# A two-layer hybrid backbone: the mixers as 570 named units, emitted in the order of a written list

## The chip, the cores and the metric

The kernel runs on one core of one Trainium2 chip. The metric is the device time of one execution, in microseconds (us), as the median of several runs; lower is better.

## What is computed

Two layers of a diffusion backbone work on 512 latent tokens and 256 context tokens of width 1024. Each layer has a mixer and a channel part, both wrapped in norms, modulation and gates:

```python
h = rmsnorm(x, norm_g[0]) * (1 + sc1[:, None]) + sh1[:, None]
qa, ka, va, qr, kr, vr, gr, z, xbc, dt = jnp.split(h @ w_in, split_idx, axis=-1)
att, att_c = attention_mixer(qa, ka, va, ...)      # 6 heads of 64, softmax over 768 keys
ret, ret_c = retention_mixer(qr, kr, vr, gr, ...)  # 4 heads, both directions, chunks of 128
ssd, ssd_c = ssd_mixer(z, xbc, dt, ...)            # 6 heads, convolution of 5 taps, chunks of 128
o = jnp.concatenate([att, ret, ssd], axis=-1) @ w_out
x = x + g1[:, None] * rmsnorm(o, norm_g[1])
h2 = rmsnorm(x, norm_g[2]) * (1 + sc2[:, None]) + sh2[:, None]
x = x + g2[:, None] * rmsnorm(squared_relu_mlp(h2, w_ff1, w_ff2), norm_g[3])
```

The context tokens go through the same steps in the first layer; in the second they only serve as keys, values and first states. All data are float32. Large products are made from three products of split operands (a high part and a rest).

## The kernel before

Tokens lie in six tiles of 128 (four latent, two context). The function `mixers(l, ...)` writes the whole mixer of one layer, and it does so in five stretches of Python code, one after the other:

- **Projections for keys and values, and the convolution.** `kvp` holds the products for attention keys, values and step sizes. Then seven groups of 128 convolution channels follow (`conv_chunk`, groups 3, 4, 5, 6, 0, 1, 2): products into `xbc`, a copy into `cin`, four taps in `acc` (L696), a tanh `th`, and for groups 0 to 4 the transposes `xt` back to tokens. `kv_post` (norm and rotation of the keys, in two halves) stands behind group 4, `decays` behind group 5.
- **State-space heads.** `ssd_head_a` makes the decay matrix `tb` of a head (scalar, vector and GpSimd work), `ssd_head_b` multiplies it (`yi`), and `ssd_state` takes one step of the state in both directions: a weighting `vw` (L784), the product with the state before (`in`), and the sums `ds` (L797). One tile of the projections `qap` and `zp` is written between the pieces.
- **Gate and norm** of the state-space output, through DRAM.
- **Attention.** For each head and pair of query tiles: scores `s`, maximum, softmax `P`, transposes `pt`, product with the values `pv`, and a store (L966). One tile of `krvp`, `qgp` or one step of the modulation `mq` (first layer only) is written after each pair.
- **Retention.** For each of four heads: transposes of keys and queries (`dTkr`, `dTqr`), scores `rs`, chunk sums `rd`, the state `rst` (a chain of ten VectorE instructions, L1050 and L1052), outputs `ry` (L1056, L1057), a group norm. Transposes of finished outputs (`sT`) and the first products of the output projection (`op`) are written between.

Memory is handed out in rings: a tag such as `t3` has four buffers, `u3` six, `m6` three, `n9` two, and PSUM has two buffers for each of `pa`, `pb`, `pc`. A tile that is written later in the code gets the next buffer of its ring when the one before is released.

All loads and stores stand on SP's queue, in order. Each engine works through its own instructions in order. That order is not simply the order in which the code writes the instructions: the compiler's planner reads what was written, with its dependencies and buffers, and puts instructions that it takes to be ready ahead of earlier ones; among ready ones, the one written first goes first.

Of the kernel before, what the change touches and what calls it, by code (L numbers as in the profile page):

```python
# [9 lines left out]
F32 = mybir.dt.float32  # L10
# [10 lines left out]
D = 1024  # L21
# [21 lines left out]
def shape_constants():  # L43
# [16 lines left out]
    # query minus key in a chunk; steps from the chunk before to a query, for both directions  # L60
# [3 lines left out]
    return cst, rel  # L64

# [15 lines left out]
def tile_hybrid_backbone(  # L81
# [120 lines left out]
    def wraw(src, shape, name):  # L202
        """one half of a unit: at most 1024 elements a partition"""
# [6 lines left out]
    def wunit(src, shape, name, lo_eng=None, pool=None):  # L210
        """src: function (first row block, row blocks) -> list of (AP, first column, columns)"""
# [13 lines left out]
    def wcols(w, k0, cols):  # L225
        """row blocks from k0 on; cols: list of (column in w, column in the unit, columns)"""
# [44 lines left out]
    def mod_cols(l, sec, q, nrow):  # L271
        """section of 512 columns of the modulation, as per-feature columns; q: [nrow, 512] in SBUF"""
# [75 lines left out]
    def mod_sums(l, sec, acc, raw=None):  # L348
        """the same, with the sums over the chunks off the tensor engine; acc [128, 2, 512]"""
# [22 lines left out]
    def cond_cols(n):  # L372
        """silu of both conditionings: [partition, chunk of 128 / n features, stream], the same on n groups of partitions"""
# [15 lines left out]
    def mod_groups(secs, acc, cs):  # L389
        """sections [(layer, section)] side by side on groups of partitions; acc [128, 2, 512]"""  # L390
# [27 lines left out]
    def gate_row(pool, l, which, stream):  # L418
        """(gate * norm_g) of one stream on every partition; which 0: mixer, 1: channel"""
# [16 lines left out]
    def modulate(q, xv, tt, l, which, hT, lo_eng=None, ks=(0, KC), cut=KC // 2):  # L436
        """q, xv [128, chunk, token]: q * A + B -> xv, and its parts into tile tt of hT"""
# [13 lines left out]
    def norm_tile(src, xh, tt, l, which, hT, lo_eng=None, half_bank=None):  # L451
        """src [128, D]; xh a scratch [128, D]; writes tile tt of hT (hi, lo)"""
# [12 lines left out]
    def mm3(o, a, b, first, last):  # L465
        """o += a^T b for split operands a = (hi, lo), b = (hi, lo)"""
# [18 lines left out]
    def tiles(pool, name, n=6):  # L485
        """tokens of tile tt: [:, tt] = [chunk, token]"""
# [14 lines left out]
    def mixers(l, mp, hT, alloc_mix, kvw=None):  # L501
# [48 lines left out]
        def rope(st, t, nh):  # L550
            """rotate st [128, nh * 64] (one tile of latent tokens) in place"""
# [7 lines left out]
        def qk_norm(q, st, t, nh, goff, ms=None):  # L559
            """q [128, nh * 64] in PSUM -> st: rmsnorm a head, gain, rotation; with ms only the sums of squares"""  # L560
# [17 lines left out]
        # ---- steps of the state-space heads, attention keys and values  # L578
# [13 lines left out]
        run(tm_group("kv", 268, [(KA, 0, 256), (DT0, 256, 12)], 6, c_kv, (pB, pC), kvw[:1]))  # L592
        if l:
            # out of the memory of the weights, once that of the mixers is free
            for i in range(2):
                G.tensor_copy(kvt[:, 3 * i : 3 * i + 3], kvr[i])
                kvr[i] = kvt[:, 3 * i : 3 * i + 3]

        def kv_post():
            for i in range(2):  # L600
                ts = slice(3 * i, 3 * i + 3)
                nc.sync.dma_start(tv(vad)[:, ts, :], kvr[i][:, :, 128:256])
                sq = t3([128, 3, 2, 64], f"sq{i}")
                kv = kvr[i][:, :, 0:128].rearrange("p t (h d) -> p t h d", d=64)
                ms = sm.tile([128, 3, 2], F32, tag="km", name=f"km{l}{i}")
                rs = sm.tile([128, 3, 2], F32, tag="kr", name=f"kr{l}{i}")
                S.activation(sq, kv, AF.Square)
                V.tensor_reduce(ms, sq, AX.X, ALU.add)
                V.tensor_scalar(ms, ms, 1.0 / 64, EPS, ALU.mult, ALU.add)
                rsqrt(rs.rearrange("p a b -> p (a b)"), ms.rearrange("p a b -> p (a b)"), 6, "kv")  # L610
                for h in range(2):
                    k = kv[:, :, h, :]
                    G.tensor_tensor(k, k, bc(par[:, P_KG : P_KG + 64], 1, 3), ALU.mult)
                    G.tensor_tensor(k, k, bc(rs[:, :, h], 2, 64), ALU.mult)
                for t in range(3 * i, min(4, 3 * i + 3)):
                    rope(kvr[i][:, t % 3, 0:128], t, 2)
                nc.sync.dma_start(tv(kad)[:, ts, :], kvr[i][:, :, 0:128])

        def mod_secs(*secs):
            if l == 0:  # L620
                for s in secs:
                    yield from (mod_whole if s in (6,7,8,9,) else mod_split)(0, s, lambda shape, name: mp.tile([128, 512], F32, tag="fcol", name=name)[: shape[0]])
# [5 lines left out]
        mods_gen = mod_secs(*range(4, 10))  # L628
# [10 lines left out]
        def decays():  # L639
            """decays of the state-space heads"""  # L640
# [3 lines left out]
            V.scalar_tensor_tensor(la, dtv, -1.0, bc(ea, 1, 6), ALU.mult, ALU.mult)  # L644
            lav = la.rearrange("p a b -> p (a b)")
# [14 lines left out]
            V.tensor_scalar(ncol, fcol[:, :, 0:12], -1.0, None, ALU.mult)  # L660
            G.memset(frow[64:128].bitcast(F32), 0.0)
# [5 lines left out]


        # ---- convolution channels
# [4 lines left out]
        cwu = {}  # L674

        def conv_chunk(j):
            on = wc or j < 5
            h, lo = cwu[j]
            cin = t3([128, 776], "cin")
            acc = t3([128, 776], "acc")  # L680
            n = 772 if on else 512
            G.memset(cin[:, 0:2], 0.0)
            G.memset(cin[:, 514:518], 0.0)
            if on:
                G.memset(cin[:, 774:776], 0.0)
            for c0, t0, t1 in ((2, 0, 512), (518, 512, 768))[: 2 if on else 1]:
                q = pB([128, 512], f"xbc{l}{j}{t0}")[:, : t1 - t0]
                qv = q.rearrange("p (t c) -> p t c", c=128)
                ts = slice(t0 // 128, t1 // 128)
                for k in range(KC):  # L690
                    mm3(qv, (h[:, k, :], lo[:, k, :]), (hh[:, ts, k, :], hl[:, ts, k, :]), k == 0, k == KC - 1)
                S.activation(cin[:, c0 : c0 + t1 - t0], q, AF.Copy)  # L692
# [13 lines left out]
            if j < 5:  # L706
                q = pA([128, 6, 128], f"xt{l}{j}")
                for t in range(6):
                    transpose(q[:, t, :], dst[:, tcol(t) : tcol(t) + 128])
                o = xs_tok[:, :, j * 128 : (j + 1) * 128] if j < 3 else b_tok[:, :, (j - 3) * 128 : (j - 2) * 128]  # L710
                S.activation(o, q, AF.Copy)

        for js in ((3, 4), (5, 6), (0, 1), (2,)):
            h, lo = kvw[1] if js[0] == 3 and len(kvw) > 1 else xbc_unit(l, js)
            for i, j in enumerate(js):
                cwu[j] = (h[:, :, i * 128 : (i + 1) * 128], lo[:, :, i * 128 : (i + 1) * 128])
                conv_chunk(j)
                if j == 4:
                    kv_post()
                if j == 5:  # L720
                    decays()

        # ---- state-space heads
# [11 lines left out]

        mats = {}

        def ssd_head_a(h):
            g = h // 3
            gf = gfb[g]  # L740
            a = t3([128, 6, 128], f"a{h}")
            for d in range(2):
                r = 6 * d + h
                qf = pA([128, 6, 128], f"F{l}{h}{d}")
                qv = qf.rearrange("p a b -> p (a b)")
                oh = onehot[:, r : r + 1].broadcast_to([128, 128])
                T.matmul(qv[:, 0:512], oh, frow[:, 0:512], start=True, stop=True)
                if wc:
                    T.matmul(qv[:, 512:768], oh, frow[:, 512:768], start=True, stop=True)
# [724 lines left out]
```

## Time and profile before

| what | us |
|---|---|
| runs | 1890.38, 1890.81, 1883.89 |
| median | 1890.38 |
| span of the profiled execution, first to last instruction | 1880.8 |
| PE busy in it | 1753.1 |
| VectorE (DVE) busy in it | 1219.7 |
| ScalarE (ACT) busy in it | 703.0 |
| GpSimd (POOL) busy in it | 369.1 |
| mean granted clock of TensorE, share of full | 0.972 |

A separate total time of the profiled execution is not recorded: its span stands for it. The lowest run is 3.1 us above that span and the median 9.6 us. Busy time is the time in which an engine has an instruction under way; matmuls are pipelined, so their records overlap and the mean duration of one is longer than the distance from one to the next. A wait is idle time of an engine just before an instruction, put down to what ended it.

### The profile page before, as it was taken

To read this page: it belongs to the slowest core of one execution; us is meant where nothing else is said; L and a number is where in the kernel's file an instruction comes from. 1 tells how busy PE (TensorE), PEld (TensorE's weight loads), DVE (VectorE), ACT (ScalarE), POOL (GpSimd) and SP (SyncE) were. 2 spreads that over 40 slices of the span, in tenths; PEclk is the share of its full clock that TensorE was granted. 3 is DMA by queue.
4 is the path that set the end of the run, shared out by engine and by line. 5 is a ranking of instruction groups with operands and counts; after the bars stand their busy time and mean duration, and the time that the engine had idled before them with its cause. 6 is when DMAs were issued, how large, how long until landed. Compare 5 with 4: busy or idle time off the path is not lost. (4 is left out here: it accounts for less than half of the span.)

```text
span 1880.8 us, 24641 instructions
## 1 busy us (share of the span) xinstructions
PE 1753.1 (93%) x8991; PEld 1443.0 (77%) x8991; DVE 1219.7 (65%) x2462; ACT 703.0 (37%) x1267; POOL 369.1 (20%) x391
## 2 busy tenths in 40 slices
PE   6987999997999999999999979888987999999998
PEld 2877977655878888888888868777866788888886
DVE  5868985664668566566566586788876654444445
ACT  5543376652461111201201275433772532222222
POOL 0047232313001100100100132553022021111112
PEclk9999999997999999999999999999996999999999
DMA  8410243366444334434434433224324432222332
GB/s 274 124 52 32 89 149 104 104 182 184 146 135 136 124 101 132 125 107 123 126 105 118 152 123 91 65 71 124 100 73 110 147 122 90 90 90 91 102 105 95
DMA packets 189078, 217.00 MB, mean 115 GB/s; under 512 B 67667, under 2 KB 142237, under 8 KB 188957
## 3 DMA queue, kind: packets, MB, share of 16 engines
q1 hardware_dynamic: 188956, 215.43, 37.8%
q8 instruction: 71, 1.16, 0.2%
q14 instruction: 51, 0.41, 0.1%
HBM read 189.66 MB, written 25.72 MB: 115 GB/s over the span
## 5 line engine op out<-in xcount | busy, mean ns | idle before, releaser
L467 PE MATMUL f<-h_h,wh_f 128*128 128x512 f32 (+1 forms) x800 | 280.3, 351 | 1.4 <-ACT h_h L448 1.4
L469 PE MATMUL f<-h_h,wl_f 128*128 128x512 f32 (+1 forms) x800 | 281.0, 352 | 0.0
L468 PE MATMUL f<-h_l,wh_f 128*128 128x512 f32 (+1 forms) x800 | 280.1, 350 | 0.8 <-DVE h_l L449 0.8
L1299 POOL TENSOR_TENSOR r<-r 128x768 f32<-128x768 f32 (+1 forms) x64 | 93.8, 1466 | 847.4 <-ACT r L1298 837.8
L467 PE MATMUL f<-wh_g,uh 128*128 128x512 f32 x640 | 253.0, 396 | 4.1 <-DVE acc L1327 1.7
L468 PE MATMUL f<-wl_g,uh 128*128 128x512 f32 x640 | 252.6, 395 | 0.0
L469 PE MATMUL f<-wh_g,ul 128*128 128x512 f32 x640 | 251.8, 394 | 0.0
L221 ACT ACTIVATE wh_f<-wr_f 128x1024 fp32r<-128x1024 f32 x64 | 66.5, 1055 | 377.2 <-PE f L469 164.4
L1329 DVE TENSOR_TENSOR acc<-acc,f 128x512 f32<-128x512 f32 x140 | 96.0, 686 | 121.0 <-PE f L469 119.6
L467 PEld LDWEIGHTS f<-h_h,wh_f 128*128 128x128 f32 x800 | 152.0, 190 | 23.0 <-ACT h_h L448 1.5
L468 PEld LDWEIGHTS f<-h_l,wh_f 128*128 128x128 f32 x800 | 151.1, 189 | 22.8 <-DVE h_l L449 1.0
L469 PEld LDWEIGHTS f<-h_h,wl_f 128*128 128x128 f32 x800 | 151.2, 189 | 20.8
L405 DVE SCALAR_TENSOR_TENSOR ga<-wr_mg,cg_a,ga 128x512 f32<-128x512 f32 x216 | 153.6, 762 | 14.6 <-DMA wr_mg<-in_w_mod_dram 14.6
L467 PEld LDWEIGHTS f<-wh_g,uh 128*128 128x128 f32 x640 | 120.1, 188 | 33.5 <-DVE acc L1327 2.2
L469 PEld LDWEIGHTS f<-wh_g,ul 128*128 128x128 f32 x640 | 120.1, 188 | 28.8
L468 PEld LDWEIGHTS f<-wl_g,uh 128*128 128x128 f32 x640 | 120.2, 188 | 27.4 <-DVE wl_g L222 0.2
L1298 ACT ACTIVATE r<-f 128x768 f32<-128x768 f32 (+1 forms) x64 | 44.8, 699 | 193.4 <-PE f L469 133.4
L1300 DVE CAST uh<-r 128x768 fp32r<-128x768 f32 (+1 forms) x64 | 32.3, 505 | 123.2 <-POOL r L1299 123.2
L222 DVE TENSOR_TENSOR wl_f<-wr_f,wh_f 128x1024 fp32r<-128x1024 f32 x64 | 77.6, 1220 | 51.3 <-ACT wh_f L221 51.3
L222 DVE TENSOR_TENSOR wl_g<-wr_g,wh_g 128x1024 fp32r<-128x1024 f32 x62 | 76.6, 1241 | 50.9 <-ACT wh_g L221 50.8
L221 ACT ACTIVATE wh_g<-wr_g 128x1024 fp32r<-128x1024 f32 x64 | 67.3, 1056 | 94.2 <-DMA wr_g<-in_w_ff_dram 53.6
L467 PE MATMUL xbc<-h_h,wh_xbc 128*128 128x512 f32 (+1 forms) x208 | 73.5, 353 | 7.7 <-ACT cin L692 7.7
(405 smaller groups left out, 3774.3 us busy)
## 6 DMA issues: line engine op xcount, KB each, us to landing
wr_f<-in_w_ff_dram SPq DMA_DIRECT2D x64, 512.0 KB, 3.7
wr_g<-in_w_ff_dram SPq DMA_DIRECT2D x64, 512.0 KB, 3.5
wr_mg<-in_w_mod_dram SPq DMA_DIRECT2D x192, 128.0 KB, 2.9
wr_m<-in_w_mod_dram SPq DMA_DIRECT2D x24, 512.0 KB, 3.8
m<-in_w_mod_dram SPq DMA_DIRECT2D x32, 256.0 KB, 4.2
wr_o<-in_w_out_dram SPq DMA_DIRECT2D x16, 512.0 KB, 4.1
wr_xbc<-in_w_in_dram SPq DMA_DIRECT2D x14, 512.0 KB, 5.3
xmid<-xt SPq DMA_DIRECT2D x10, 512.0 KB, 2.6
```

What stands on the lines that cost most here:

```text
L221: S.activation(hv[:, a0 : a0 + an], r, AF.Copy)
L222: (lo_eng or V).tensor_tensor(lv[:, a0 : a0 + an], r, hv[:, a0 : a0 + an].bitcast(F32), ALU.subtract)
L405: V.scalar_tensor_tensor(acc[:, s], r2[:, k % 2], w, acc[:, s], ALU.mult, ALU.add)
L467: T.matmul(o, a[0], b[0], start=first, stop=False)
L468: T.matmul(o, a[0], b[1], start=False, stop=False)
L469: T.matmul(o, a[1], b[0], start=False, stop=last)
L1298: S.activation(r, q[:, :NT], AF.Relu)
L1299: G.tensor_tensor(r, r, r, ALU.mult)
L1300: V.tensor_copy(uh, r)
L1329: V.tensor_tensor(acc[tt][:, ns], acc[tt][:, ns], qs[tt][half], ALU.add)
```

## The change

`mixers` no longer runs its stretches as it comes to them. Each piece of work becomes a unit with a name, a function and the names of the units that it must follow. After all units are declared, a list in the file gives the order, and one loop calls them. The pieces are smaller than before: `kv_post` is cut in two (`kp0`, `kp1`), the decays in three (`de`, `ds`, `dr`), a convolution group in products (`xa`, `xb`), taps (`xc`) and transposes (`xt`), a state-space step in weighting, product and sums for each direction (`sv`, `si`, `sd`), a decay matrix in `f`, `f`, `m`, an attention tile in scores with softmax (`as`) and transposes (`at`), a pair's product with the values (`ao`), and a retention head in loads (`rl`), transposes (`rp`), centring (`rx`), scores (`rs`), sums (`rd`), state (`rt`), outputs (`ro`), gain (`rg`) and norm (`rn`). `us`, `ua`, `ur` are the transposed outputs, `wp` and `wo` the first weights and products of the output projection, `md` the steps of the modulation. There is also a function `default_plan` with an order made by loops, which is used only if a layer has no list; both have one. The core of the diff:

```diff
+ATT_N9 = True
+PLAN = {
+    0: """
+        kv0 kv1 kv2 kv3 kv4 kv5 xw3 xa3 xb3 xc3 xt3 xa4 xb4 xc4 kp1 xw5 xa5 xb5 xc5 de xw0 xt4 kp0
+        xa0 ds xb0 xc0 xa1 xb1 xc1 xw2 xt0 dr xa6 xb6 xc6 xa2 xt1 xb2 xc2 xt2 qa0 f10 g0 f11 m1 qa1
+        sv00 sv01 sd01 f00 g1 f01 m0 sk b0 qa2 f20 f21 qa3 sd00 m2 sv10 si10 qa4 f30 sd10 sv11 si11
+        sd11 f31 b1 m3 qa5 sv20 si20 sd20 sv30 sv21 si21 b2 zz0 sd21 sv31 f40 f41 m4 si30 sd30 zz1
...
+        sg1 sg2 sg3 sg4 sg5 sn av aqs rc ak0 aq0 aq1 as00 at00 as01 at01 kr0 as02 ao00 at02 as03
...
+        as44 at44 at42 at43 as45 at45 ao41 md1 ao42 rw0 as50 at50 as51 at51 md2 ao50 rl0 md3 as52
+        at52 as53 at53 md4 as54 at54 ao51 as55 at55 ao52 md5 mx rv rp0 rx0 ryt rw1 rl1 rx1 rs0 rp1
+        rd0 md6 md7 md8 md9 md10 us0 us2 rt0 md11 md12 md13 md14 md15 rg0 ro00 md16 md17 md18 rd1
+        md19 md20 us1 ro01 ro02 md21 md22 md23 rn0 rt1 rx2 rg1 rs1 rw2 rl2 rp2 ro10 ua0 md24 ro11
+        ro12 rn1 ur0 rw3 rl3 rp3 rx3 rs2 rd2 ua1 rt2 rg2 ro20 ua2 ro21 ro22 wp rs3 rn2 rd3 wo0 wo1
+        rt3 rg3 wo2 wo3 ro30 ro31 wo4 wo5 ro32 rn3 ur1
+    """.split(),
+    1: """
+        kv0 kv1 kv2 kv3 kv4 kv5 km0 km1 xw3 xa3 xb3 xa4 xc3 xb4 xt3 xc4 xw5 xa5 kp1 xc5 de xa6 xt4
+        ds kp0 xc6 xw0 xa0 dr xa1 xb0 xb1 xc0 xt0 xc1 xt1 xw2 xa2 xb2 xc2 xt2 g0 f00 f10 f11 f01 m0
+        g1 qa0 qa1 m1 sv01 sd01 sv00 sd00 sk b0 qa2 f20 f21 sv11 b1 qa3 sv10 sd11 sd10 m2 zz0 f30
...
+        at53 ao51 mx rv rl0 rx0 rp0 ryt rw1 rl1 rp1 rx1 rd0 rg1 us0 rs0 rt0 rg0 ro00 us1 ro01
+        rn0 rw2 rl2 rp2 rx2 rs1 rd1 rt1 ro10 ua0 ro11 rx3 us2 rn1 ur0 rw3 rl3 rp3 rs2 rd2 rg2 ua1
+        rt2 rs3 ro20 ua2 ro21 rn2 wp rd3 wo0 wo1 rg3 wo2 rt3 ro30 wo3 wo4 wo5 ro31 rn3 ur1
+    """.split(),
+}
...
+        UNITS, AFTER = {}, {}
+
+        def unit(name, f, *after):
+
+            UNITS[name] = f
+            AFTER[name] = [n for n in after if n]
...
+                if i < 5:
+                    unit(f"sv{i}{d}", lambda i=i, d=d: ssd_vw(i, d), *xts, "ds", f"sd{i - 1}{d}" if i else None)
+                if has_in:
+                    unit(f"si{i}{d}", lambda i=i, d=d: ssd_in(i, d), f"sd{i - 1}{d}", "sk", "xc5", "xc6")
+                    ssd_done.append(f"si{i}{d}")
...
+        plan = PLAN.get(l) or default_plan(l, NQ, nmod)
+        assert sorted(plan) == sorted(UNITS), (set(plan) ^ set(UNITS), len(plan))
+        seen = set()
+        for n in plan:
+            assert all(a in seen for a in AFTER[n]), (n, [a for a in AFTER[n] if a not in seen])
+            UNITS[n]()
+            seen.add(n)
```

## Rows read from the trace of the kernel before

**Rows 1.** The page: span, and each engine's busy time, share and instructions.

```profile
span 1880.8 us, 24641 instructions
PE 1753.1 (93%) x8991; PEld 1443.0 (77%) x8991; DVE 1219.7 (65%) x2462; ACT 703.0 (37%) x1267; POOL 369.1 (20%) x391
```

**Rows 2.** Busy time by stretch: length, engines, PEclk, DMA share, GB/s; the mixers.

```profile
48.00:148.00 100.00, 93.39 (x570) 83.78 (x569) 74.98 (x157) 48.55 (x90) 29.06 (x53) 0.98 0.29 87
148.00:240.00 92.00, 80.25 (x469) 76.20 (x470) 81.22 (x234) 33.45 (x77) 42.94 (x39) 0.96 0.24 72
240.00:398.00 158.00, 150.00 (x817) 111.05 (x815) 107.66 (x246) 108.37 (x230) 45.17 (x46) 1.00 0.40 116
398.00:470.00 72.00, 58.63 (x295) 36.71 (x293) 41.35 (x117) 21.33 (x36) 18.90 (x19) 0.86 0.69 197
...
1105.00:1219.00 114.00, 93.46 (x547) 83.12 (x545) 85.22 (x178) 56.47 (x102) 43.56 (x63) 0.94 0.27 84
1219.00:1296.00 77.00, 67.27 (x368) 61.60 (x369) 64.46 (x190) 28.26 (x60) 35.00 (x32) 0.96 0.31 90
1296.00:1408.00 112.00, 101.11 (x570) 83.09 (x568) 86.84 (x180) 78.48 (x158) 25.84 (x36) 0.95 0.32 92
1408.00:1466.00 58.00, 45.83 (x236) 40.67 (x237) 39.19 (x126) 14.57 (x30) 13.96 (x14) 0.71 0.38 94
```

**Rows 3.** Waits of PE over the span: total us, times, longest.

```profile
PE ry L1057 <- DVE rst L1052: 17.4, 6, 6.2
...
PE ds L797 <- DVE vw L784: 10.3, 6, 2.7
PE nps L152 <- ACT tt L454: 10.0, 2, 7.8
PE xbc L467 <- ACT cin L692: 7.7, 3, 5.7
PE yi L769 <- POOL tb L760: 7.3, 2, 3.7
PE xt L152 <- DVE th L705: 6.6, 3, 3.7
PE s L938 <- ACT P L944: 6.0, 4, 2.8
PE pt L152 <- DVE P L949: 3.6, 3, 1.5
...
PE mq L325 <- DMA wr_m<-in_w_mod_dram: 2.1, 4, 1.1
```

**Rows 4.** PE in order of time, retention of layer 0: start, us, what.

```profile
406.52 1.52 PE L1039 MATMUL rd<-vrr,W 128*128 128x64 f32 x12
...
451.78 1.06 PE L1039 MATMUL rd<-vrr,W 128*128 128x64 f32 x4
...
459.43 0.69 PE L1057 MATMUL ry<-rst,q 128*128 128x64 f32 x2 [6.16 <-DVE rst L1052]
```

**Rows 5.** Busy time by stretch: three stretches with a lowered clock.

```profile
120.00:140.00 20.00, 16.28 (x93) 14.41 (x92) 12.29 (x12) 9.63 (x14) 3.74 (x5) 0.91 0.17 46
...
447.00:467.60 20.60, 13.79 (x63) 12.85 (x61) 12.84 (x33) 5.99 (x9) 7.03 (x8) 0.50 0.43 138
1416.50:1450.70 34.20, 25.96 (x122) 24.04 (x120) 24.73 (x81) 8.17 (x16) 12.50 (x12) 0.55 0.43 104
```

**Rows 6.** VectorE in order of time: a constant of retention.

```profile
84.91 0.17 DVE L978 TENSOR_SCALAR lg<-nlg 128x8 f32<-128x8 f32 x1
```

**Rows 7.** Waits of PE, 398 to 470 us.

```profile
PE ry L1057 <- DVE rst L1052: 8.7, 2, 6.2
```

**Rows 8.** Waits of SP's queue over the span.

```profile
SPq L966 <- DVE fo L965: 92.3, 21, 10.3
```

**Rows 9.** Line 167 from 1165 us on (ns, least/middle/most), and POOL in time.

```profile
L167 DVE SCALAR_TENSOR_TENSOR kr<-rq_t,kr x6: 156/166/1771, 1171.6 to 1184.3; 128x6 f32<-128x6 f32 x6
...
1183.79 2.26 POOL L222 TENSOR_TENSOR wl_qa<-wr_qa,wh_qa 128x768 fp32r<-128x768 f32 x1
```

More of the change, by code (lines that the diff above doesn't have):

```diff
@@ L593, in mixers, with kv_move @@
+        for t in range(6):
+            unit(f"kv{t}", steps(kv_gen), f"kv{t - 1}" if t else None)
+        def kv_move(i):
+            G.tensor_copy(kvt[:, 3 * i : 3 * i + 3], kvr[i])
+            kvr[i] = kvt[:, 3 * i : 3 * i + 3]
         if l:
             for i in range(2):
[L596 to L617, printed above, removed]
@@ L624, in chain @@
+        for i in range(2):
+            unit(f"kp{i}", lambda i=i: kv_post(i), f"km{i}" if l else f"kv{3 * i + 2}")
         def chain(*gens):
@@ L626, in chain, with mod_gen @@
                 yield from g
-        mods_gen = mod_secs(*range(4, 10))
+        nmod = 0
+        if l == 0:
+            def mod_gen(sec):
+                row = lambda shape, name: mp.tile([128, 512], F32, tag="fcol", name=name)[: shape[0]]
+                yield from (mod_whole if sec >= 6 else mod_split)(0, sec, row)
+            mods_gen = chain(*[mod_gen(sec) for sec in range(4, 10)])
+            nmod = 6 * 4 + 1
         dtv = mp.tile([128, 6, 12], F32, tag="dtv", name=f"dtv{l}")
@@ L666, in decays @@
             V.tensor_tensor(frow[32:64], q[32:64], frow[32:64].bitcast(F32), ALU.subtract)
+        unit("de", decays, "kv5")
+        unit("ds", decay_sums, "de")
+        unit("dr", decay_rows, "ds")
         BT, CT = {}, {}
@@ new lines, in ssd_vw, with ssd_in @@
+        def ssd_vw(i, d):
+            t = orders[d][i]
+            vws[d] = s1([128, 6, 64], "vw")
+            V.tensor_tensor(vws[d], v3(xs_tok[:, t]), bc(wst[:, t, 6 * d : 6 * d + 6], 2, 64), ALU.mult)
+        def ssd_in(i, d):
+            t = orders[d][i]
+            q = pC([128, 6, 64], f"in{l}{d}{i}")
+            for g in range(2):
+                T.matmul(f2(q[:, 3 * g : 3 * g + 3, :]), CT[g][:, tcol(t) : tcol(t) + 128],
+                         f2(sst[d][:, 3 * g : 3 * g + 3, :]), start=True, stop=True)
+            yv = v3(y_tok[:, t])
+            for h in range(6):
+                V.scalar_tensor_tensor(yv[:, h, :], q[:, h, :], expf[:, t, 6 * d + h : 6 * d + h + 1], yv[:, h, :],
+                                       ALU.mult, ALU.add)
@@ new lines, in ssd_ds @@
+        def ssd_ds(i, d):
+            t, st = orders[d][i], sst[d]
+            q = pC([128, 6, 64], f"ds{l}{d}{i}")
+            for g in range(2):
+                T.matmul(f2(q[:, 3 * g : 3 * g + 3, :]), b_tok[:, t, g * 128 : (g + 1) * 128],
+                         f2(vws[d][:, 3 * g : 3 * g + 3, :]), start=True, stop=True)
+            if i == 0:
+                S.activation(st, q, AF.Copy)
+            else:
+                for h in range(6):
+                    V.scalar_tensor_tensor(st[:, h, :], st[:, h, :], dec[:, t, 6 * d + h : 6 * d + h + 1], q[:, h, :],
+                                           ALU.mult, ALU.add)
@@ L864, in mixers, with ssd_gate @@
         G.memset(ssq, 1.0)
-        for t in range(NQ):
+        def ssd_gate(t):
             sz = s1([128, 384], f"sz{t}")
@@ new lines, in att_o @@
+        def att_o(h, tp):
+            k0, nk = (0, 6) if tp < 2 else (4, 2)
+            PT = PTs[h, tp]
+            main, other = (slice(64, 128), slice(0, 64)) if h % 2 else (slice(0, 64), slice(64, 128))
+            o = pC([128, 256], f"pv{l}{h}{tp}")
+            for kt in range(nk):
+                for j in range(2):
+                    T.matmul(o, AT["v"][:, k0 + kt, h // 3, :], PT[kt // 3][:, j, kt % 3, :], start=kt == 0 and j == 0,
+                             stop=kt == nk - 1 and j == 1)
+            f = s1([128, 256], f"fo{h}{tp}")[main]
+            S.activation(f, o[other], AF.Copy)
+            V.tensor_tensor(f, f, o[main], ALU.add)
+            nc.sync.dma_start(attd[h * 64 : (h + 1) * 64, tp * 256 : (tp + 1) * 256], f)
@@ L1065, in ret_head @@
             V.tensor_reduce(var, sq, AX.X, ALU.add)
-            if True and h == 3:
+            if h == 3:
                 rsqrt_mean(rs, var, "gn", 64, NQ)
@@ new lines, in mixers, with wo_load @@
+        WP = {}
+        def wo_load():
+            WP["p"] = wout_units(l, (0,))
+            WP["g"] = wout_begin(l, MX["m"], WP["p"], 6)
+        unit("wp", wo_load, "mx")
+        ready = ["us0", "us1", "us2", "ua0", "ua1", "ua2"]
+        for i in range(6):
+            unit(f"wo{i}", lambda: next(WP["g"], 0), f"wo{i - 1}" if i else "wp", *ready[: i + 1])
+        plan = PLAN.get(l) or default_plan(l, NQ, nmod)
+        assert sorted(plan) == sorted(UNITS), (set(plan) ^ set(UNITS), len(plan))
```

585 lines of the change are left out of this document (355 added, 230 removed).

## The prediction

> **What bounds the kernel now.** I read the page first, then a table of busy time by stage, then the waits of TensorE, and last single stretches in order of time. The page shows TensorE busy for 93% of the span, VectorE for 65% [rows 1]. The chain that ended last covers only the final microseconds of the kernel, so it says nothing about the mixers. The edit touches nothing but the mixers of the two layers. In the table by stage [rows 2] these are eight rows: projections and convolution, state space, attention, retention, once for each layer. Read the busy column of PE against the length. Lengths: 100 + 92 + 158 + 72 + 114 + 77 + 112 + 58 = 783 us. PE busy: 93.4 + 80.3 + 150.0 + 58.6 + 93.5 + 67.3 + 101.1 + 45.8 = 690 us. So 93 us are without a matmul, and this is all that an order can win from idle time. VectorE is at 81.2 of 92 us and 64.5 of 77 us in the two state-space stages: there it is as near to its limit as TensorE is, and leaves 10.8 and 12.5 us.
>
> The list of waits [rows 3] splits the idle time by cause. The largest in the mixers are the retention state (`ry` on `rst`, 17.4 us), the state-space sums (`ds` on `vw`, 10.3), the convolution input (`xbc` on `cin`, 7.7), the decay matrices (`yi` on `tb`, 7.3), the convolution transposes (`xt` on `th`, 6.6) and the softmax tiles (`s` on `P` 6.0, `pt` on `P` 3.6). The `nps` row (10.0) belongs to the norm between the layers, which the list does not hold.
>
> Idle time costs a second time. Just ahead of a 6.16 us wait, in a stretch with a low clock, four `rd` matmuls take 1.06 us, where twelve take 1.52 us at the full clock earlier on: 0.265 against 0.127 us each [rows 4]. The table of stretches with a low clock [rows 5] has the granted clock of both retention tails at 0.50 and 0.55, that is at or close to 1.2 GHz, with 13.8 and 26.0 us of PE busy. At 2.4 GHz about half of these 39.8 us, 19.9, would do.
>
> **What the change does, part by part.** No instruction is added or removed that I can find: each unit holds the lines that stood in the loop, and `kv_post`, the decays, the state step and the attention head are only cut into pieces. So every engine's busy time stays but for what waits inside an instruction, and the whole effect is order. The order written down is also not the order of execution: the retention constants, written after the code of attention, run at 84.9 us among the work on the first convolution channels [rows 6], more than 150 us ahead of the attention. The compiler's planner pulls ready work forward, and the list only sets who is first. I therefore cost each part by the waits in which the list puts other TensorE work between producer and consumer, or takes it away.
>
> 1. Convolution transposes. In layer 0 the transposes of channel group 0 followed its convolution. The list puts group 1's projections ahead of them, and leaves those of groups 6 and 2 behind them as cover. The longest of the three waits for them is the one of layer 0, 3.7 us [rows 3]. Each projection has 48 matmuls; at that stage's 93.39 / 570 = 0.164 us each [rows 2] they are 7.9 us of cover. The 20 us in which this wait falls had a granted clock of 0.91 [rows 5]: 0.09 x 20 = 1.8 us of clock, which I count as saved too. Gain 5.5, bounds 0 and 6.6 + 1.8 = 8.4.
>
> 2. State-space sums. Before, `vw`, the inter-chunk product and `ds` stood together for one direction. In the list some 6 of 10 pairs in each layer have another unit's matmuls between the `sv` and the `sd`. 6/10 of 10.3 is 6.2; VectorE, the late producer, is nearly full there, so I take 6 and no clock. Bounds 0 and 10.3. The first `b` unit still follows its `m` closely: the 7.3 us for `tb` I leave at 7.3.
>
> 3. Retention. In layer 0 the sums and the state of head 1 move forward into head 0's part, ahead of head 1's scores. The waits for the state in layer 0 are two, 8.7 us, the longer one 6.2 [rows 7]; the shorter one, 2.5, is that of head 1 and goes. The long one stays, since `rd2 ua1 rt2 rg2 ro20` stands as the loop had it. In layer 1 `rs3` now stands between `rt2` and `ro20`: eight score matmuls, 1.0 us at the 0.127 us of an `rd` matmul [rows 4]. Gain 3.5, bounds 0 and 17.4.
>
> 4. Attention. The list writes the scores of a later tile ahead of the transposes and the product of an earlier one, and mixes heads at the end of a head. Of the 9.6 us on `P` I take half, 4.8; bounds 0 and 9.6. The second projection groups and the modulation keep their places within a few units.
>
> 5. Keys, values and convolution input. `kp0` moves behind the convolution of group 5, which thins the VectorE and POOL work around the `cin` wait of layer 1. I take 2, bounds 0 and 7.7.
>
> 6. DMA. Every load moves with its unit on SP's queue, where `ao` stores stand at the head waiting for `fo` for 92.3 us in 21 times [rows 8]; a later `ao` holds back the loads behind it. What has hidden this is the three weight buffers; where the cover was missing TensorE waited 2.1 us for `wr_m` [rows 3]. The list brings the loads of retention head 0 forward in layer 0 (`rl0` before the last attention tiles). I set this at nothing, between a loss and a gain of 2.1.
>
> 7. New waits. An order that moves some 500 units also makes neighbours that were apart. I allow one wait like that for `tb`, 3.6 us (half of 7.3), with one clock dip of 1.8: a loss of 5.4. Bounds 0 and 28, below.
>
> Sum: 5.5 + 6 + 3.5 + 4.8 + 2 + 0 - 5.4 = 16.4 us. Against the profiled execution (span 1880.8 us [rows 1]) that is 1864.4 us. The median of the runs is 1890.38, 9.6 above that span, and I take the same saving from it: 1874.0 us, 0.9% faster.
>
> **A place where order and lock meet.** A step of the Newton chain (L167, 128x6) takes 0.166 us in the middle case and 1.771 us in the worst; the worst starts at 1184.3 us, inside POOL's 2.26 us split of a weight at 1183.8 [rows 9]. So VectorE lost 1.6 us because of what POOL happened to do. The Trainium skill, SBUF — State Buffer, Summary: rules for kernel authors, says that of a GpSimd instruction and a VectorE one with two SBUF inputs the second to start blocks until the first is done; the trace agrees. By that rule a new order draws a new set of such collisions, which speaks against any gain counted wait by wait.
>
> **Rivals.**
> - *Nothing to measure.* The planner undoes the list: [rows 6] speaks for it, and so does VectorE's 84 to 88% in the state-space stages, where a filled hole only moves. Against it: the retention tail and the convolution are not full on any engine. Time 1881 to 1900.
> - *Slower, by collisions.* POOL's ropes, masks and splits meet other VectorE chains than before, at 1.6 us for each meeting on a chain for which TensorE waits. The time passes 1900 when the 16.4 are eaten and another 9.5 lost: 26 / 1.6 = 16 more meetings, over eight stages two in each. With all of the gains and 28 us of it, 1902; without the gains and with half of it, 1904. For it: rows 9. Against it: the waits of TensorE in the mixers are mostly single ones below 4 us, and much of VectorE's work reads PSUM. I give 1905.
> - *Much faster.* The retention state is hidden in full and TensorE keeps 2.4 GHz in both tails: 17.4 - 3.5 = 13.9 more, and the 19.9 of the clock: 16.4 + 33.8 = 50.2, time 1840. Against it: `rt2` stands where it stood.
>
> **How the numbers follow.** Forecast (1850 to 1881): 0.46. Much faster (below 1850): 0.14. Nothing to measure: 0.22. Slower: 0.18. The bound of 0.5%, 9.5 us, is about what a measurement of this kernel can tell from no change; the three runs shown spread over 6.9 us. So faster 0.60, same 0.22, slower 0.18. The range takes the forecast, nothing, and most of the much faster case, and leaves out about one in ten at either end: 1842 to 1903. The forecast's own range is 1858 to 1881.
>
> **What would show it.** Same counts of instructions on each engine. The waits `xt` on `th` and `ds` on `vw` fall to about half of 16.9 together; `ry` on `rst` falls from 17.4 to about 14; the `nps` wait stays. The 783 us of mixers become about 766, and the other stages keep their lengths within 2 us. I am wrong if the list of waits is of the same size under other names (nothing), if many short VectorE instructions show a worst case near 1.8 us (slower), or if the retention tails keep the full clock (much faster).

## The result, and the profile after

The changed kernel takes 1862.56 us (median of 4 runs, 1859.15 to 1864.61) against 1888.18 us for the kernel before beside it: a ratio of 0.9862, 95% interval 0.9841 to 0.9884. It is 25.6 us faster. The profiled execution took 1859.15 us. The page of it, the same two lines as [rows 1]:

```profile
span 1857.4 us, 24648 instructions
PE 1752.8 (94%) x8991; PEld 1440.8 (78%) x8991; DVE 1207.3 (65%) x2462; ACT 703.0 (38%) x1267; POOL 370.4 (20%) x391
```

The counts are those of before, and TensorE's busy time too (1752.8 against 1753.1 us). VectorE's is not: with the same 2462 instructions it is 12.4 us less, 9.0 of them in the mixers. A new order should not change how long an instruction takes, so this line is the first clue. (The two lists name 321 and 252 units, 573 in all and not 570.)

For the stages I no longer cut by the clock but by events, so that the same work is compared: the first `kvp` product, the start of the last group of `xt` transposes, the first `dTka`, the first `dTkr`, and the end of the last `sT`. Below they are called convolution, state space, attention and retention. The table of busy time by stretch, change, four rows for each layer (columns as in [rows 2]):

```profile
43.20:144.90 101.70, 96.21 (x582) 83.80 (x582) 81.15 (x169) 53.06 (x100) 29.36 (x56) 1.00 0.31 91
144.90:222.50 77.60, 71.71 (x430) 69.30 (x430) 68.33 (x214) 29.49 (x71) 40.18 (x35) 0.98 0.20 59
222.50:381.50 159.00, 151.58 (x831) 113.69 (x829) 109.90 (x257) 108.94 (x227) 48.01 (x49) 1.00 0.45 129
381.50:471.00 89.50, 78.86 (x431) 52.27 (x432) 60.08 (x163) 29.65 (x51) 19.12 (x18) 0.96 0.63 181
1085.40:1195.50 110.10, 92.95 (x542) 82.79 (x540) 83.78 (x179) 55.94 (x102) 42.45 (x62) 0.94 0.29 86
1195.50:1263.90 68.40, 62.94 (x344) 57.39 (x345) 59.14 (x184) 26.08 (x56) 34.86 (x31) 0.98 0.32 94
1263.90:1377.00 113.10, 104.65 (x601) 84.63 (x600) 86.95 (x185) 81.48 (x162) 25.17 (x37) 0.97 0.33 96
1377.00:1446.70 69.70, 57.60 (x256) 50.33 (x255) 43.03 (x134) 15.17 (x30) 14.59 (x14) 0.61 0.31 78
```

Four rows of the kernel before, cut by the same events: state space of layer 0, and state space, attention and retention of layer 1.

```profile
148.20:233.80 85.60, 74.05 (x430) 70.64 (x431) 75.36 (x215) 29.53 (x71) 40.55 (x35) 0.96 0.18 55
...
1219.10:1287.90 68.80, 59.17 (x314) 54.17 (x315) 57.25 (x164) 24.92 (x54) 33.85 (x30) 0.95 0.30 88
1287.90:1408.30 120.40, 109.52 (x625) 90.81 (x625) 93.95 (x204) 82.12 (x163) 26.90 (x37) 0.96 0.32 93
1408.30:1470.30 62.00, 49.83 (x256) 43.87 (x255) 41.30 (x134) 15.38 (x31) 13.96 (x14) 0.72 0.36 88
```

The lengths side by side, with those of three experiments that are told below:

| stage | before | loops (e1) | change | list for convolution and state space (e12) | list for attention (e11) |
|---|---|---|---|---|---|
| layer 0: convolution | 104.8 | 106.0 | 101.7 | 102.7 | 105.9 |
| state space | 85.6 | 85.5 | 77.6 | 77.7 | 85.5 |
| attention | 165.0 | 163.5 | 159.0 | 164.8 | 164.2 |
| retention | 90.8 | 95.4 | 89.5 | 91.2 | 92.0 |
| layer 1: convolution | 114.0 | 114.3 | 110.1 | 110.0 | 111.9 |
| state space | 68.8 | 69.2 | 68.4 | 68.0 | 69.3 |
| attention | 120.4 | 121.8 | 113.1 | 113.8 | 120.5 |
| retention | 62.0 | 63.4 | 69.7 | 62.7 | 63.9 |
| sum | 811.4 | 819.1 | 789.1 | 790.9 | 813.2 |

Of the 23.4 us by which the span fell, 22.3 are in the mixers: 18.4 in layer 0 and 3.9 in layer 1, where retention gives back 7.7. In the state space of layer 0 TensorE has the same 430 matmuls in both kernels and the stage is 8.0 us shorter; VectorE's busy time in it falls by 7.0 us, its idle time only from 10.2 to 9.3. The granted clock rose from 0.96 to 0.98, which is worth at most 0.04 x 85.6 - 0.02 x 77.6 = 1.9 us. The 8.0 us are far above the scatter: with all of GpSimd's work in place the stage is 77.5 to 77.7 us in every run that has the list's order there, and 85.5 to 86.1 in every run that has not. In layer 1's attention the row of before has 625 matmuls and the row of after 601: some work is no longer in this stage, and the experiments show whose it is.

The waits of TensorE over the span (total, times, longest), change:

```profile
PE nps L274 <- ACT tt L576: 10.1, 2, 7.8
...
PE ry L1305 <- DVE rst L1295: 9.0, 4, 5.5
PE yi L940 <- POOL tb L931: 6.2, 3, 2.7
PE xbc L589 <- ACT cin L842: 3.9, 3, 2.0
PE s L1140 <- DVE qla L1095: 3.9, 3, 1.7
PE xt L274 <- DVE th L861: 3.9, 4, 1.4
PE qap L589 <- ACT cin L842: 3.4, 2, 2.8
PE s L1140 <- ACT P L1146: 3.3, 6, 1.0
...
PE F L914 <- DVE gfb L898: 3.1, 2, 1.8
...
PE ds L973 <- DVE vw L956: 1.6, 2, 0.9
```

Against [rows 3], `ry` on `rst` is halved, `xt` on `th` fell from 6.6 to 3.9, `s` on `P` from 6.0 to 3.3, and `ds` on `vw` from 10.3 to 1.6. `nps` and `tb` stayed. New or grown beside them: `s` on `qla` (1.2 us before), `qap` on `cin` (1.6 before), `F` on `gfb`.

### The profile page after: what moved, and what is told of

It is laid out like the page before. It is cut to its first block, busy times and chain, and to the rows that moved or that the text cites. A ratio compares the mean times of both kernels' runs of the same rounds, so it can differ in the third digit from the quotient of the medians.

```text
span 1857.4 us, 24648 instructions
## 1 busy us (share of the span) xinstructions
PE 1752.8 (94%) x8991; PEld 1440.8 (78%) x8991; DVE 1207.3 (65%) x2462; ACT 703.0 (38%) x1267; POOL 370.4 (20%) x391
## 5 line engine op out<-in xcount | busy, mean ns | idle before, releaser
L527 DVE SCALAR_TENSOR_TENSOR ga<-wr_mg,cg_a,ga 128x512 f32<-128x512 f32 x216 | 151.2, 752 | 12.5 <-DMA wr_mg<-in_w_mod_dram 12.4
L344 DVE TENSOR_TENSOR wl_f<-wr_f,wh_f 128x1024 fp32r<-128x1024 f32 x64 | 77.6, 1221 | 50.8 <-ACT wh_f L343 50.7
```

The source lines that it names most:

```text
L344: (lo_eng or V).tensor_tensor(lv[:, a0 : a0 + an], r, hv[:, a0 : a0 + an].bitcast(F32), ALU.subtract)
L527: V.scalar_tensor_tensor(acc[:, s], r2[:, k % 2], w, acc[:, s], ALU.mult, ALU.add)
```

## Experiments

**Theories.** A: the parts of the prediction are right, each wait that falls is won. B: the order mainly changes how VectorE and GpSimd get in each other's way, and the waits are where TensorE feels it. C: the cutting into units does something by itself.

**e1: the units, without the list.** Both layers take the order of the loops.

```diff
+PLAN = {}
```

> Units as in the change, but both layers in the order of default_plan, that is of the loops before. If the gain comes from the order alone: within 0.5% of before, about 1888 us, layer 0's mixer 441 us long (kvp to the last sT) and layer 1's 365. If cutting the code into units gave part of it (buffers handed out at other moments): clearly below, 1875 or so.

Measured: 1890.39 us, 1.0009 (0.9992 to 1.0025). C is out, and the list carries the whole change. This kernel is a second copy of the order of before; its retention of layer 0 is 95.4 us against 90.8. Over all eight runs with the loops' order in that stage it is 90.4 to 95.4 us, so a single stage at the low clock varies by some 5 us, and smaller differences between two executions say nothing there.

**e2 and e3: the list in one layer.**

```diff
+PLAN = {0: PLAN[0]}      # e2
+PLAN = {1: PLAN[1]}      # e3
```

> The list for layer 0, the loops' order for layer 1. Read from the two traces the list shortens layer 0's mixer by 18 us and layer 1's by 4: 1870 us. If the layers were alike, as the prediction had it, 1876; if the layers depend on each other, the two single gains don't add up to 25.6.

> The list for layer 1 only. From the traces: 4 to 5 us faster than before, 1884 us, with projections, state space and attention about 11 us shorter and the retention about 8 us longer at a low clock. If the low clock of the retention came from what layer 0 did, the tail would be as before here and the gain 12 us: 1876.

Measured: 1870.21 us, 0.9912 (0.9885 to 0.9939), and 1879.85 us, 0.9951 (0.9934 to 0.9968). The gains are 0.88% and 0.49%, together 1.37%, and the change's is 1.38%. The layers add up. About two thirds come from layer 0. The first time was as expected, the second was not: 1884 us or 1876 were named, and the gain is twice the 4 to 5 us that the two traces gave for layer 1. In e3's own trace state space and attention of that layer are 179.3 us, against 189.2 before, and its tail is 67.1 against 62.0.

**e4: the list for everything but retention.** Retention goes in the order of the loops.

```diff
+def mixed(l, listed):
+    loops = default_plan(l, (6, 4)[l], (25, 0)[l])
+    return [n for s in range(4) for n in (PLAN[l] if s in listed else loops) if stage(n) == s]
+PLAN = {l: mixed(l, (0, 1, 2)) for l in range(2)}
```

> The list for everything but the retention, which has the order of the loops in both layers. If the list's retention order in layer 1 is what costs 8 us: layer 1 gains 11, layer 0 loses its 1: about 1856, faster than the change. If the tail's low clock follows from any order in which PE has little left to do there: the same as the change, 1862.

Measured: 1863.65 us, 0.9872 (0.9845 to 0.9898). The second theory has it: step 3 of the prediction is worth nothing that shows in the total. The tail of layer 1 is back at 64.2 us here, yet the kernel is no faster for it: layer 0's attention and retention together take 257.3 us, against 248.5 in the change.

**e5: steps 1 and 2 alone.** The order of the loops, with the products and taps of channel group 1 ahead of the transposes of group 0, the products of group 2 ahead of the transposes of group 1, and each `sv` well ahead of its `sd`.

```diff
+    for n in ("xw2", "xa1", "xb1", "xc1"):
+        ahead(p, n, "xt0")
+    for n in ("xa2", "xb2"):
+        ahead(p, n, "xt1")
+    for i in range(5):
+        ahead(p, f"sv{i}0", f"f{i + 1}0" if i < 4 else "f50")
+        ahead(p, f"sv{i}1", f"si{i}0" if f"si{i}0" in p else f"sd{i}0")
```

> The loops' order with two parts of the list alone, in both layers: the convolution transposes of groups 0 and 1 behind the next group's projections, and the weightings vw ahead of the next head's decay matrices. If a wait falls because other TensorE work stands between producer and consumer (steps 1 and 2 of the prediction): xt on th falls from 6.6 to about 2, ds on vw from 10.3 to 2, projections and state space of layer 0 together about 8 us shorter, 1878 us in all. If VectorE sets the pace there and what the list won is VectorE time (its busy time in the state space of layer 0 fell from 75.4 to 68.3 us): the named waits fall but others take their place, and the time stays within 0.3% of before.

Measured: 1878.33 us, 0.9944 (0.9924 to 0.9963). This is the total of the first theory, but not by the parts that it named. (The profile is of the longest of the nine runs, 1885.47 us, so the lengths of its stages may be a little high.) The waits of TensorE, e5:

```profile
PE F L934 <- DVE gfb L918: 8.6, 2, 4.5
PE xt L294 <- DVE th L881: 8.0, 5, 2.9
...
PE in L982 <- DVE y_tok L986: 6.6, 5, 2.8
```

The wait `ds` on `vw` went from 10.3 to 2.0 us, just as step 2 has it, but the state space of layer 0 is 86.1 us, no shorter than 85.5. In its place `F` on `gfb` and `in` on `y_tok` appeared: all of them VectorE's products, in a stage in which VectorE is at 74 of 86 us. What was moved forward on a nearly full engine made something else late. In layer 1 state space and attention are 184.0 us against 191.0 in e1, so there the move did help. And `xt` on `th` did not fall (5.3 us in layer 0's convolution, 5.2 in e1); it was cut into three pieces with a longest of 2.9 instead of 3.7, and the granted clock of that stage rose from 0.97 to 1.00, its length from 106.0 to 103.3 us. TensorE's busy time for the same 582 matmuls fell by 2.4 of these 2.7 us. Step 1's gain is there, and in e5 it is the clock's and not the wait's.

**e6 and e7: GpSimd unloaded.** Gain and rotation of the attention queries, which GpSimd computes beside the state space, are left out, in the order of the loops (e6) and of the list (e7); the queries enter attention without them.

```diff
-            G.tensor_tensor(v3(st), v3(st), bc(par[:, goff : goff + 64], 1, nh), ALU.mult)
-            if t < 4:
-                rope(st, t, nh)
```

> The loops' order; the GpSimd work on the attention queries (gain and rotation, five of the nine kinds of GpSimd instructions of the state-space stage) is left out. Taken with the next run. If the list won VectorE time by letting GpSimd and VectorE meet less often: VectorE's busy time in the state space of layer 0 falls here from 75 towards 70 us, the stage from 85.6 to about 80, and the gap to the list shrinks from 8 to 3 us or less. If cover for TensorE is what counts: VectorE's busy time hardly moves and the gap stays near 8.

> The list for both layers, with the same work left out as in the run before. State space of layer 0: 77.6 us with the work; by the meetings about 76, by cover 75 or less, that is as far below the loops as with the work.

Measured: e6 1863.38 us, 0.9877 (0.9848 to 0.9907); e7 1853.46 us, 0.9813 (0.9794 to 0.9832). So the list is worth 9.9 us without this GpSimd work (1863.38 to 1853.46), and 25.6 with it. The state space of layer 0, by stretch, e6 and then e7:

```profile
147.70:222.60 74.90, 70.32 (x430) 67.53 (x430) 68.81 (x216) 29.70 (x72) 25.34 (x17) 1.00 0.19 59
```

```profile
143.90:217.50 73.60, 70.16 (x431) 67.78 (x431) 65.77 (x214) 29.27 (x72) 24.51 (x17) 1.00 0.19 58
```

Taking 15 us of work from GpSimd, which was busy for 40 of 85 us, shortened the stage by 10.6 us in the order of the loops and by 4.0 in that of the list. Between the two orders 1.3 us are left of 7.9. So in layer 0's state space the list's gain is nearly all a matter of where GpSimd's work lies. (The 73.6 us of e7 are below both numbers that its expectation names; by the gap, its reason for them, the meetings have it.) In layer 1 it is not: state space and attention together are 183.0 us (e6) and 177.0 (e7), a gap of 6.0, against 191.0 and 181.5 with the rotation, a gap of 9.5.

How GpSimd does it is to be seen in the groups of VectorE instructions in that stage (line, operation, tiles, shape, count, busy us, mean ns): before, change, e6.

```profile
L759 DVE SCALAR_TENSOR_TENSOR tb<-gfb,dtv,tb 128x128 f32<-128x128 f32 x36 | 17.1, 536 | 2.3 <-POOL tb L757 2.3
L792 DVE SCALAR_TENSOR_TENSOR y_tok<-in,expf,y_tok 128x64 f32<-128x64 f32 x48 | 10.0, 272 | 1.0 <-PE in L788 1.0
...
L754 DVE SCALAR_TENSOR_TENSOR a<-F,ncol,a 128x128 f32<-128x128 f32 x36 | 9.8, 338 | 0.0
L784 DVE TENSOR_TENSOR vw<-xs_tok,wst 128x384 f32<-128x384 f32 x10 | 8.7, 880 | 1.4 <-POOL st_qa L570 1.4
```

```profile
L930 DVE SCALAR_TENSOR_TENSOR tb<-gfb,dtv,tb 128x128 f32<-128x128 f32 x36 | 14.7, 476 | 1.3 <-POOL tb L928 1.3
L921 DVE SCALAR_TENSOR_TENSOR a<-F,ncol,a 128x128 f32<-128x128 f32 x36 | 10.1, 340 | 0.0
...
L956 DVE TENSOR_TENSOR vw<-xs_tok,wst 128x384 f32<-128x384 f32 x10 | 6.8, 700 | 1.4 <-POOL st_qa L692 1.4
```

```profile
L930 DVE SCALAR_TENSOR_TENSOR tb<-gfb,dtv,tb 128x128 f32<-128x128 f32 x36 | 12.9, 422 | 0.1
...
L921 DVE SCALAR_TENSOR_TENSOR a<-F,ncol,a 128x128 f32<-128x128 f32 x36 | 9.8, 340 | 0.0
```

PSUM holds the results of matmuls, SBUF the other tiles of this kernel. Compare `tb` and `a`. They have the same operation, shape and count. `a` reads `F` from PSUM, and takes 338, 340 and 340 ns. `tb` reads `gfb` and itself, both in SBUF, and takes 536, 476 and 422. Instructions that read PSUM (`a`, and `y_tok` at 272 ns) are the same in these kernels. From before to the change the 7.0 us lie in four groups that read two tiles of SBUF: `tb` 2.4 and `vw` 1.9 as shown, `st_zt` 1.8 (with one instruction fewer in the stretch) and the first `y_tok` 0.9. In e6 `vw` stays long, at 825 ns: GpSimd's own products for `tb` are still there.

The durations of `tb` in that stage before, least, middle and most, and those of GpSimd's product that writes `tb` first:

```profile
L759 DVE SCALAR_TENSOR_TENSOR tb<-gfb,dtv,tb x36: 335/342/1566, 158.1 to 220.6; 128x128 f32<-128x128 f32 x36
L757 POOL TENSOR_TENSOR tb<-gfb,dtv x6: 1483/1602/1677, 156.6 to 210.4; 128x768 f32<-128x768 f32 x6
```

So the middle `tb` takes as long as `a`, and the mean of 536 comes from a few that take up to 1566 ns, about as long as one GpSimd product. Two cases in order of time, from e1, VectorE and then GpSimd:

```profile
166.95 4.08 DVE L933 SCALAR_TENSOR_TENSOR tb<-gfb,dtv,tb 128x128 f32<-128x128 f32 x5
...
179.47 1.97 DVE L959 TENSOR_TENSOR vw<-xs_tok,wst 128x384 f32<-128x384 f32 x1
```

```profile
165.55 0.59 POOL L679 TENSOR_TENSOR rp<-st_qa,cst 128x192 f32<-128x192 f32 x1
166.10 0.59 POOL L680 TENSOR_TENSOR rp<-st_qa,cst 128x192 f32<-128x192 f32 x1
166.77 1.00 POOL L681 TENSOR_TENSOR st_qa<-st_qa,cst 128x384 f32<-128x384 f32 x1
167.85 1.01 POOL L682 TENSOR_TENSOR st_qa<-st_qa,rp 128x384 f32<-128x384 f32 x1
168.82 1.53 POOL L931 TENSOR_TENSOR tb<-gfb,dtv 128x768 f32<-128x768 f32 x1
...
179.23 1.80 POOL L934 TENSOR_TENSOR tb<-tb,a 128x768 f32<-128x768 f32 x1 [1.34 <-DVE tb L933]
```

Five `tb` take 4.08 us while GpSimd runs a rotation and a product back to back; a `vw` that takes 0.55 us in the middle case takes 1.97 us, and ends 0.4 us after the GpSimd product beside it. The Trainium skill, SBUF — State Buffer, Summary: rules for kernel authors, has it that a VectorE instruction with two SBUF inputs and a GpSimd one that reads SBUF exclude each other, the second waiting until the first is done, and that whichever is off the critical path should be scheduled around the other. These rows agree with it. The prediction used this rule against the change. It acts in both directions.

Two more ways are open to e6's saving. GpSimd also makes `tb` itself, and a rotation ahead of it on GpSimd's queue makes it late: the wait `yi` on `tb` is 7.3 us before and 6.2 in the change, but 2.2 in e6. And `vw` waits 1.4 us for GpSimd's work on `st_qa` before it starts, before and in the change alike, but not in e6. For the list's own 8.0 us both are small, since VectorE's idle time in the stage hardly fell; for the 10.6 us of e6 they are not separated from the blocking.

**e8: layer 1's tail filled.** The list, with three products of 128x512 per head behind the state in layer 1's retention, whose result is not read: 12 more matmuls.

```diff
+            if l:
+                dm = pB([128, 512], f"dm{h}")
+                for _ in range(3):
+                    T.matmul(dm, rw[h][:, 0:128], rw[h][:, 384:896], start=True, stop=True)
```

> The change with twelve more matmuls in the retention of layer 1: three of 128x512 for each head, on data at hand, whose result nobody reads, behind the state chain's start. They add 12 us of TensorE work at the full clock and 24 at half. If the tail of layer 1 (69.7 us, 54.6 of them at half clock) is long because TensorE's short waits keep its clock down: the granted clock rises above 0.8 there, the tail is not longer than 70 us and may be shorter, 1855 to 1863 us in all. If the state chain on VectorE alone sets the length: the clock may rise, the tail stays. If TensorE's work sets it at any clock: the tail is 10 to 20 us longer, 1875.

Measured: 1866.53 us, 0.9883 (0.9859 to 0.9906), not told apart from the change. Of the change's retention in layer 1, the part at the low clock, and three matmuls of it in order of time:

```profile
1382.90:1437.50 54.60, 44.76 (x182) 39.89 (x183) 35.48 (x112) 10.71 (x21) 14.59 (x14) 0.50 0.31 76
```

```profile
1420.53 0.69 PE L1305 MATMUL ry<-rst,q 128*128 128x64 f32 x2 [5.48 <-DVE rst L1295]
...
1435.41 0.63 PE L591 MATMUL op<-wh_o,mix_l 128*128 128x512 f32 x1
...
1437.99 0.39 PE L591 MATMUL op<-wh_o,mix_l 128*128 128x512 f32 x1
```

For 54.6 us without a break the granted clock is 0.50, that is 1.2 GHz; the same 128x512 product takes 0.63 us in it and 0.39 us behind it. In e8 the retention row is:

```profile
1384.10:1447.70 63.60, 56.53 (x278) 42.33 (x276) 43.73 (x134) 15.00 (x31) 13.97 (x14) 0.84 0.34 86
```

There are 22 more matmuls in the row, in 63.6 instead of 69.7 us, at a mean clock of 0.84 instead of 0.61. The new ones account for all of them: the trace has 24 records for the 12 products. Half of full speed means that what is missing to 1 counts twice: the time at 1.2 GHz fell from 2 x 0.39 x 69.7 = 54 us to 2 x 0.16 x 63.6 = 20 us. With the clock up and more work in it the tail is 6.1 us shorter than in the change, and 3.5 to 6.1 shorter than in the three runs that have the list's order there unfilled (67.1 to 69.7 us). I read this as the least that the low clock costs here. But behind the tail 6.5 us came back, from the last `sT` to the end (410.7 us in the change, 417.2 in e8); 3.6 of them are the norm's wait `nps` on `tt`, 5.9 us instead of 2.3. Why the rest is longer I can't say. So the first theory holds for the tail and not for the total, which was to be 1855 to 1863 us.

**e9 and e10: other orders for layer 1's retention.** e9 takes the list but for this one stage, which goes as in the loops. e10 takes an order of my own, with the state of each head ahead of the outputs of the head before.

```diff
+PLAN[1] = mixed(1, (0, 1, 2))                          # e9
+T1 = """mx rv rl0 rx0 rp0 ryt rw1 rd0 rt0 rl1 rx1 rs0 rp1 rg0 rd1 us0 ro00 ro01 rt1 rs1 rg1 rn0 rw2 rl2 rx2
...
+PLAN[1] = PLAN[1][: PLAN[1].index("mx")] + T1          # e10
```

> The list in layer 0 whole and in layer 1 up to the attention; retention of layer 1 in the order of the loops (rt2 after two outputs of head 1, no rs3 ahead of ro20). Theory, the list's retention order in layer 1 is itself worse and costs the clock: the tail of layer 1 falls from 69.7 to about 62 us, half clock in it from 54.6 to about 34 us, total 1855 +- 3. Rival, the tail's clock varies from execution to execution and the order is of no account: tail 64 to 70 us, total 1861 +- 3.

> The list everywhere, but the retention of layer 1 in an order of my own: transposes, scores, sums and state of head h+1 stand ahead of the outputs of head h, so that the ten-step state chain has a head's scores and outputs as cover. Theory, the state wait is what empties TensorE in this tail and the empty time is what takes its clock: the two long waits for rst in layer 1 (2.9 and 5.5 us) fall under 1 us each, the tail goes from 69.7 to 60 to 63 us, half clock in it under 30 us, total 1854 +- 3. Rival 1, the tail is short of matmuls for VectorE's whole work and any order has the low clock: tail 66 to 70 us, total 1861 +- 3. Rival 2, what is saved in the tail is given back behind it, as with the filled tail: tail 62 us, total 1861 +- 3.

Measured: e9 1862.14 us, 0.983 (0.9788 to 0.9872); e10 1864.83 us, 0.9857 (0.9819 to 0.9895). Neither is told apart from the change. e9's tail is 65.7 us, and tail and total lie in the range of its rival, that the order is of no account. The rows of all runs speak against this rival all the same: the tail of layer 1 is 67.1 to 69.7 us in the three unfilled ones with the list's order there, and 60.4 to 65.7 us in the nine with the loops'. The list's order costs this tail some 5 us, but in e9 the total does not show them; in its profiled execution layer 0's retention took 94.7 us, 5.2 more than in the change with the same order. In e10 the wait for `rst` has left the list of waits, and the tail did not notice. Its row:

```profile
1380.20:1448.20 68.00, 56.13 (x246) 48.71 (x245) 39.63 (x134) 15.25 (x31) 14.16 (x14) 0.60 0.32 79
```

So the state's wait is not what keeps this tail long, and my theory of it falls; the tail is that of rival 1. Other waits stand there, of 2.8 us for a load (2.0 in the change), 2.6 for `mix_l`, 2.4 for `W` and 2.1 for `ry`, and the clock stayed at 0.60.

**e11 and e12: attention alone, and convolution with state space alone.** The same `mixed` as in e4, with `(2,)` and with `(0, 1)`.

> The loops' order but for attention, which has the list's in both layers. Theory, attention's gain is its own (scores of a later tile ahead of transposes): layer 0 from 164 to 158 us, layer 1 from 121 to 113, total 1889 - 13 = 1876 +- 3. Rival, the attention stage is shorter under the list because work was moved out of it into other stages or because it begins in another state: both within 2 us of the loops, total 1888 +- 3.

> The list's order for convolution and state space in both layers, the loops' order for attention and retention. Theory, the whole gain is made in these two stages, and what looked like a gain of attention in layer 1 (121 to 113 us) is state-space work (the last in and yi with their VectorE sums) that no longer hangs over into attention: layer 1's attention falls to about 113 us though its own order is the loops', layer 0's stays at 163 to 166, total 0.988 of the kernel before, 1867 +- 4. Rival, attention's order is worth something as soon as the state-space work is out of its way: layer 1's attention 117 us or more, total 1874 or more.

Measured: e11 1886.86 us, 0.9979 (0.9955 to 1.0002); e12 1864.18 us, 0.9879 (0.9846 to 0.9911). State space and attention of layer 1 in e12, where attention has the order of the loops:

```profile
1207.20:1275.20 68.00, 61.96 (x345) 55.82 (x346) 60.12 (x184) 26.15 (x56) 34.08 (x31) 1.00 0.31 95
1275.20:1389.00 113.80, 104.44 (x601) 86.02 (x600) 85.90 (x185) 80.97 (x162) 25.66 (x37) 0.97 0.33 95
```

Attention is 113.8 us long, as under its own list. Counted by name, some 25 matmuls are missing against the loops: eight `yi` and four `in` of the state space and 13 `krp` projections. Before, they ran in attention, the first two with their VectorE sums; now they lie in a state-space stage with 345 matmuls instead of 314 that is no longer than it was. Attention's list alone does nothing that e11 can tell from no change (at most 0.45%, the end of its interval), and the list for convolution and state space alone is as fast as the whole list within the intervals.

## Why the prediction came out as it did

The time was right, at 1862.56 us within the range and near the lower end of the forecast's own. Its sum was 16.4 us and 25.6 were measured. That the sum came this near is in part luck, since its errors lie on both sides: steps 3 and 4 hold 8.3 us that the totals do not show, step 2 is some 9 us too small, and the 5.4 us that step 7 takes away were not lost. By its steps:

1. *Convolution transposes* (5.5 forecast). The convolution stages are 2 to 4 us shorter in each layer, in the change and in e12. e5 shows that the moved products bring 2.7 us in layer 0 with the wait as long as before but broken up: there the clock was nearly all, where the step had 3.7 for the wait and 1.8 for the clock. In the change itself the wait in that stage fell too, from 5.1 to 2.6 us, while the stage became 3.1 us shorter; the two parts are not separated there. The size is about right.
2. *State-space sums* (6 forecast). This is the step that was mis-sized, and its mechanism was wrong in layer 0. State space with what hung over from it is shorter by some 8 us in layer 0 and 7 in layer 1: 85.6 to 77.7, and 68.8 + 120.4 to 68.0 + 113.8 in e12. The step took VectorE's work as fixed, with its near-full row as a limit on the gain. But that row held the blocking by GpSimd: VectorE's busy time in layer 0's state space fell from 75.36 to 68.33 us with one instruction fewer in the stretch. In e5 the named wait was taken away in layer 0, and the stage kept its length. In layer 1 the step's mechanism fits: the same move brought 7.0 us there, of the 9.5 between the loops (e1) and the list.
3. *Retention* (3.5 forecast). The wait fell by 8.4 us and not 3.4, and not where the step had it: in layer 0 it went from 8.7 to 0.4 us, with the long one that was to stay, and in layer 1 it stayed (8.7 and 8.6). It brought nothing to the total: e4 and e12 have the loops' retention and are as fast. Taking attention and retention together, since the cut between them moves (the `mq` steps), layer 0 takes 248.5 to 254.7 us in the six runs with the list's order for both and 254.0 to 260.9 in the eight with the loops' retention: some 5 us won. Layer 1's tail loses about as much (e9), and in the change it runs at 1.2 GHz for 54 of 69.7 us. That the one makes up for the other is read from these rows; no total shows it. The rival *much faster* needed both tails at the full clock; layer 0's came near it (0.96 in the change, 0.91 to 0.94 in the five other runs with this order), layer 1's went the other way.
4. *Attention* (4.8 forecast). Wrong. The waits on `P` fell from 9.6 to 5.5 us, about as told, yet e11 gives 0.2%, with an interval that includes no change.
5. *Keys, values, convolution input* (2 forecast). `xbc` on `cin` fell from 7.7 to 3.9 us, but `qap` on `cin` rose from 1.6 to 3.4. It lies within the convolution's gain and was not tried by itself.
6. *DMA* (nothing). Nothing was seen of it; `mq` on `wr_m` fell from 2.1 to 1.3 us.
7. *New waits* (a loss of 5.4). They came: `qla` grew by 2.7, `qap` by 1.8 and `gfb` by 3.1 us. But the term had its sign from the belief that a new draw of collisions costs, and its upper bound of 28 us is nowhere worked out. The rival *slower, by collisions* named the right mechanism with the wrong sign: the loops' own draw was a poor one, and with the same instructions VectorE is busy for 9.0 us less in the mixers.

The rival *nothing to measure* rested on the planner undoing the list. e2, e3 and e12 show that it does not. What it rested on as well, that a filled hole only moves, holds for step 2 in layer 0 and for step 4, each taken by itself.

What stays open: how much of e6's saving is blocking, and how much is `tb` late on GpSimd's queue; how the gain of layer 1's state space divides, of whose 9.5 us 6.0 remain without the rotation; and what sets the length of layer 1's retention, which neither a hidden state (e10) nor filled holes (e8) turned into a shorter total. No version with all of its work in place is told apart from the change as a faster one.

## What to carry to other kernels

Before you call an engine full, ask whether its busy time holds waiting: compare the mean of an instruction that reads two SBUF tiles with its own middle case, here 536 against 342 ns, and with its like that reads PSUM, here 338. If the mean is higher, look at what GpSimd does during the long ones; order, or less GpSimd work, can buy the time back, as it did in layer 0's state space. A wait in the list need not be worth its length: where the engine that ends it is nearly full, as in that stage of e5, taking the wait away moved it.

## What was not expected of the hardware

GpSimd is busy for a fifth of the span and stands ahead of few of TensorE's waits, and yet 38 us less of its work in the mixers (254.8 us in e1, 217.0 in e6) made the kernel 1.2% faster than before, about 23 us. And a stretch of 54.6 us stayed at 1.2 GHz although no wait of TensorE in it was longer than 5.5 us; the clock came back amid a row of 128x512 products.
